# S5 woven with HGRN, retention last, and the output projection's rows parted to match

## The chip, the cores and the metric

The kernel runs on one core of one Trainium2 chip. The metric is device time in microseconds: three runs of the kernel before took 3756.23, 3757.74 and 3765.32 us, median 3757.74. One further execution was profiled; it took 3765.03 us.

## The reference

Two layers of a hybrid block over 256 context and 1024 latent tokens of width 1024, in float32. Each layer normalizes, projects once, runs four mixers in both directions on 256 channels each, projects their joined outputs back, and ends with an MLP:

```python
pc, pl = split_cols(hc @ w_in), split_cols(hl @ w_in)
a_c, a_l = hgrn2_mixer(pc[0], pl[0], lb, hg_norm_g)
r_c, r_l = retention_mixer(pc[1], pl[1], ret_log_gamma, pos_c, pos_l)
g_c, g_l = gdn_mixer(pc[2], pl[2], rows, conv_w, a_log, dt_bias, gdn_norm_g)
s_c, s_l = s5_mixer(pc[3], pl[3], lam_re, lam_im, log_dt, b_re, b_im, c_re, c_im, d_skip, glu_w, glu_b)
y_l = jnp.concatenate([a_l, r_l, g_l, s_l], axis=-1) @ w_out
y_c = jnp.concatenate([a_c, r_c, g_c, s_c], axis=-1) @ w_out if need_ctx else None
```

The second layer needs no context output (`need_ctx` is false there). HGRN is gated linear attention in chunks of 16 with a decay for each channel. Retention turns q and k by rope, attends within chunks of 64 (joined to 128 here) with a fixed decay and carries a state. S5 is a complex diagonal scan over 16 groups of 16 channels; its sum over both directions goes through GELU and a gated linear unit. Gated delta (gdn) is the fourth.

## The kernel before, in words

Everything is transposed: channels on the 128 partitions, tokens along the free axis. The joined mixer output `a` is 8 rows of 128 channels in HBM: rows 0 and 1 are HGRN's, 2 and 3 retention's, 4 and 5 gated delta's, 6 and 7 S5's. A float32 product is made of three passes over a high and a low half (hi x hi, lo x hi, hi x lo), so a product over n rows takes 3n matmuls.

A mixer is a Python generator that writes its instructions in pieces. `piped` runs the segments of one mixer one piece apart, and `weave(a, b, n, c, m)` writes a piece of a, then n of b, then m of c. Program order is only a wish: a scheduler with a model of the engines puts the instructions of each engine in their final order, by priority and by when it thinks the inputs are there. Each engine then runs its queue in that order, and so does SyncE (SP), which issues nearly all DMAs.

In each layer, when the projection is done, the order is: the end of gated delta (`gdn_out`) woven with HGRN, retention (`ret`) woven with HGRN, S5 alone (`s5`), and the rest of HGRN and of the modulation (lines 1963 to 1971). `gdn_out` and `ret` share one pool of tiles (`rtp`), HGRN has its own on the right side, and S5's pool lies in the outer region `sl`. The modulation products (`mod`, 256 KB weight loads each) are woven in between.

`ret` works on segments of 256 tokens, five of them. It first loads its tables (`rt_tb`, line 335). Stage 1 loads v, x, a copy of x with swapped halves in four DMAs (`rt_xs`, line 356), and rope tables; ropes k on VectorE and GpSimd (lines 358 to 360), stores it, transposes it (372), scales it (377), multiplies it with v (386) into the states `rt_S`, which `chain` then scans (401). When all of stage 1 is done, stage 2 ropes q, multiplies q and k (422), masks (424), and adds products with v and with the states (434, 437); `gnorm` normalizes, gates and stores the rows of `a` (lines 71 to 112).

`s5` works in four quarters. A quarter loads tables of 1.15 MB, multiplies the inputs by them (`s_px`, 1365), turns them (1371 to 1375), scans (1380), turns back (1384 to 1395), and multiplies again (`s_py`, 1403 and 1405). After every second quarter come transposes (1422, 1429) and GELU (1441 to 1445); at the end the gated unit (1454 to 1460) and the stores.

The output projection is in two parts. Part 1 (low priority, `hiprio` down) loads six rows of `a` (`load_a`, tile `at`, line 1756), splits them (1757, 1758), and runs 8 x 3 groups of 18 matmuls (layer 1: 8 x 2) into `wo_ps`; each group adds the residual (1781) and stores to `xs`. Part 2 (called "few") does the two rows that are left with 6 matmuls a group on top of `xs`, and leads on to the norm and the MLP. Two lists, `rowsA` and `rowsB`, give the order in which the input projection makes its 128-column blocks; 'r' and 's' stand for retention's v and S5's input.

Of the kernel before, what the change touches and what calls it, by code (L numbers as in the profile page):

```python
# [146 lines left out]
def hgrn(k, l, need_ctx):  # L147
# [27 lines left out]
    def stage1(sg):  # L175
# [15 lines left out]
        if full:  # L191
# [8 lines left out]
            AD = tp.tile([128, 8, 64], F32, name='hg_ad', tag='hg_ad', bufs=2)  # L200
            A = tp.tile([128, 8, 2, 64], F32, name='hg_A', tag='hg_A', bufs=1)
            yield
# [3 lines left out]
        for li, s in enumerate((1, 2, 4, 8, 16, 32, 64)):  # L206
            nb = 256 // s
            if full:
# [5 lines left out]
                else:  # L214
                    for x in range(2):
                        nc.scalar.activation(A[Y2[x], :, 1 - x], ps[Y2[x]], AF.Copy)
                        nc.vector.tensor_copy(A[Y2[x], :, x], AD[Y2[x]])
# [1499 lines left out]
def within(k, gen, tp, tag):  # L1717

    while True:
        k.tp, k.mxt = tp, (tag, k.nps[tag])  # L1720
        try:
            next(gen)
        except StopIteration:
            return
        yield


def weave(a, b, n, c=(), m=0):

    for _ in a:  # L1730
        for _ in range(n):
            next(b, None)
        for _ in range(m):
            next(c, None)


def run(gen):
    for _ in gen:
        pass
# [128 lines left out]
def program(k):  # L1868
    from contextlib import ExitStack
    nc, tc = k.nc, k.tc  # L1870
    with ExitStack() as es:
        pool = lambda st, name, **kw: st.enter_context(tc.tile_pool(name=name, bufs=1, **kw))
        near = lambda st, name, **kw: pool(st, name, reuse_waits='tile', **kw)
# [60 lines left out]
        for l in range(2):  # L1934
            need = l == 0
            blocks = ALL if need else LAT
            xsrc = k.I['xT'] if l == 0 else xs
            k.mml = ('mm', 'mm', 'mo')
            k.g = {}
            k.rows_done.clear()  # L1940
            k.wpool, k.ecm = k.balance[0]
            k.filler = proj_steps(k, l, H, k.rowsA, need)
            drain(k)
            k.filler = proj_steps(k, l, H, k.rowsB, need)
            with ExitStack() as st:
                gv, gc, su, tb = (near(st, f'{n}{l}') for n in ('gv', 'gc', 'su', 'tb'))
                with hi():
                    for i, _ in enumerate(within(k, gdn_conv(k, l, need, gc, gv), su, 'mx')):
                        if i == k.statat:
                            gdn_stats(k, l)  # L1950
                    if l == 0:
                        hg_params(k)
                    run(within(k, s5_tables(k, l), tb, 'mc'))
            with ExitStack() as st, hi():
                gs, fp = near(st, f'gs{l}'), near(st, f'gf{l}')
                run(within(k, gdn_main(k, l, need, fp), gs, 'mx'))
            drain(k)
            hs.close()
            hs = ExitStack()
            k.wpool, k.ecm = k.balance[1]  # L1960
            with ExitStack() as sl, ExitStack() as sr, hi():
                with ExitStack() as sh:
                    hg = within(k, hgrn(k, l, need), near(sh, f'hg{l}', side='right'), 'mx')
                    with ExitStack() as st:
                        rtp = near(st, f'rt{l}')
                        mod = (x for i, r in k.mods[l] for x in modulation(k, i, r, k.wp, (('w_hi', 'w_lo'), k.wb[1], 4)))
                        weave(within(k, gdn_out(k, l, need), rtp, 'mc'), hg, k.ratios[0], mod, k.mr[0])
                        weave(within(k, ret(k, l, need), rtp, 'mc'), hg, k.ratios[1], mod, k.mr[1])
                    weave(within(k, s5(k, l, need), near(sl, f's5{l}'), 'mc'), hg, k.ratios[2], mod, k.mr[2])
                    run(hg)  # L1970
                    run(mod)
                with ExitStack() as sa, tc.high_priority(offset=-k.hiprio):
                    wa = near(sa, 'wa', side='right')
                    k.mml = k.womm
                    pair = lambda: [wa.tile([128, T], F32R, name=n, tag='h', bufs=12) for n in ('ahi', 'alo')]
                    A = load_a(k, l, (4, 5, 2, 3, 0, 1), wa, k.nwa, blocks, pair)

                    def start(m, b0, bn):
                        x = wa.tile([128, 512], F32, name='xp', tag='t2', bufs=k.nwa)[:, :bn]
                        nc.sync.dma_start(x, xsrc[m, :, b0:b0 + bn])  # L1980
                        return x
                    run(w_out(k, l, A, blocks, start, lambda m, b0, bn, x: nc.sync.dma_start(xs[m, :, b0:b0 + bn], x)))
            k.hp = near(hs, f'hp{l}', side='right')
            k.mml = DENSE
            with ExitStack() as st:
                k.xp = k.np_ = near(st, f'ml{l}')
                t0 = blocks[0][0]
                Xt = [k.xp.tile([128, T], F32, name=f'x{i}') for i in range(8)]
                X = lambda kt: Xt[kt]
                part = lambda m, b0, bn: Xt[m][:, b0:b0 + bn]  # L1990
                pair = lambda: [k.xp.tile([128, T], F32R, name=n, tag='hid', bufs=k.nhid) for n in ('ahi', 'alo')]
                A = load_a(k, l, (6, 7), k.xp, k.nt2, blocks, pair)
                for b0, bn in blocks:
                    for kt in range(8):
                        nc.sync.dma_start(Xt[kt][:, b0:b0 + bn], xs[kt, :, b0:b0 + bn])
                new_acc = lambda: k.xp.tile([128, T], F32, name='nr_acc', tag='hid', bufs=k.nhid)
                acc = [new_acc()]
                H = [hpair(k) for _ in range(8)]

                def done(m, b0, bn, x):  # L2000
                    square(k, acc[0], x, m, b0, bn)
                    if m == 7:
                        norm_mod(k, X, acc[0], l, 3, b0, bn, H)
                run(w_out(k, l, A, blocks, part, done, True))
                if k.mods[2 + l]:
                    k.mml = DENSE2
                    k.filler = (x for i, r in k.mods[2 + l] for x in modulation(k, i, r, k.xp, ('w_mo', 2, 1)))
                H2 = [hpair(k) for _ in range(8)] if l == 0 else None

                def final(m, b0, bn):  # L2010
                    k.mml = DENSE
                    if (m, b0) == (0, t0):
                        acc[0] = new_acc()
                    sl = slice(b0, b0 + bn)
                    if m is not None:
                        square(k, acc[0], Xt[m][:, sl], m, b0, bn)
                        return
                    if l == 0:
                        norm_mod(k, X, acc[0], 1, 0, b0, bn, H2)
                        return  # L2020
                    rb = rnorm(k, acc[0], b0, bn)
                    for kt in range(8):
                        u = k.np_.tile([128, 512], F32, name='nm_u', tag='t2', bufs=k.nt2)[:, :bn]
                        nc.vector.scalar_tensor_tensor(u, Xt[kt][:, sl], k.vecs[:, 128 + kt:129 + kt], rb[:, :bn],  # L2024
                                                       op0=MULT, op1=MULT)
                        nc.sync.dma_start(k.O[kt, :, b0 - TC:b0 - TC + bn], u)
                mlp(k, l, H, X, blocks, final)
                if l == 0:
                    for kt in range(8):
                        nc.sync.dma_start(xs[kt], Xt[kt])  # L2030
                H = H2
# [7 lines left out]
def tune(k):  # L2039
    k.nps = dict(mm=2, mx=3, mc=2, mo=1)  # L2040
    k.nmc = 2
    k.mods = (((0, 1), (0, 2), (1, 0)), ((1, 1), (1, 2)), (), ())
    k.xat = 0
    k.bm = False
    k.gA, k.gM, k.gT, k.gQ = 3, 3, 2, 3
    k.nln, k.nvs = 3, 1
    k.hiprio = 6000
    k.convfirst = False
    k.cut = 8
    k.ratios = (1, 1, 1)  # L2050
    k.mr = (0, 1, 1)
    k.hlag = 9
    k.nw0 = 8
    k.parts = (1, 1)
    k.womm = ('mm', 'mx', 'mo')
    k.backat = 0
    k.rowsA = [16, 14, 17, 15, 'h', 18, 19]
    k.rowsB = ['r', 10, 11, 8, 9, 12, 13, 2, 3, 4, 5, 0, 1, 20, 21, 6, 7, 's']
    k.npace = {}
    k.lowprio = 8000  # L2060
    k.chainprio = 2000
    k.wb = (3, 4)
    k.nt2 = 5
    k.sqp, k.nva, k.nlp = (1, 4), (0, 2, 4, 6), (1, 3, 4, 5, 7)
    k.nz = 6
    k.nwa = 8
    k.balance = ((1, 4), (3, 4))
    k.nhid = 6
    k.ncv, k.ntk, k.statat = 4, 3, 3
    k.nv = (2, 2)  # L2070
    k.mods = (((0, 1), (0, 2), (1, 0)), ((1, 1), (1, 2)), (), ())
    k.hlag = 8
    k.nlp = (2, 4, 6)
# [29 lines left out]
```

## Time and profile before

| | us |
|---|---|
| median of three runs | 3757.74 (3756.23 to 3765.32) |
| profiled execution | 3765.03, its span 3763.2 |
| TensorE busy over the span | 3351.4 (89%) |
| VectorE, ScalarE, GpSimd | 2089.8, 1115.8, 1149.9 |
| HGRN woven with retention | 665 to 872 and 2591 to 2800 |
| S5, with part 1 of the output projection | 872 to 1059 and 2800 to 2978 |
| part 2, norm, first MLP matmuls | 1059 to 1131 and 2978 to 3034 |

In the rows below, a stretch lists for each engine its busy time and its instructions in brackets, in the order TensorE, its weight load, VectorE, ScalarE, GpSimd; then the mean granted TensorE clock (1 is 2.4 GHz), the busy share of the DMA engines and GB/s. A group of instructions gives line, engine, operation, output and input, shapes and count, then busy time and mean duration, and behind the second bar the engine's idle time ahead of it and what ended it. SPq is SyncE's queue.

### The profile page before, as it was taken

The numbers are of one execution on the slowest core, as the hardware profiler recorded it, in microseconds if no ns is written. First come the engines' busy times: TensorE is split into PE (matmuls) and PEld (weight loads), VectorE is DVE, ScalarE is ACT, GpSimd is POOL, SyncE is SP. The second block draws the span as 40 slices with busy tenths as digits, with TensorE's granted clock in tenths as the row PEclk, the third lists the DMA queues.
The fourth block names the chain that finished last, engine by engine and source line by source line (L and its number), as shares of the span: only waits on it lengthen the run. The fifth ranks groups of instructions, "written<-read, shape, count | busy, mean of one in ns | idle before, by whom it ended". The sixth has DMA issues, their size and how long they took to land. (4 is left out here: it accounts for less than half of the span.)

```text
span 3763.2 us, 59989 instructions
## 1 busy us (share of the span) xinstructions
PE 3351.4 (89%) x23367; PEld 2718.6 (72%) x23367; DVE 2089.8 (56%) x3927; ACT 1115.8 (30%) x1991; POOL 1149.9 (31%) x1198
## 2 busy tenths in 40 slices
PE   5888999787879999999998886997678599999997
PEld 3777788555758888888886775776457478888886
DVE  9978521885664433443447977413956654344445
ACT  5333221663143112112114342213542232222222
POOL 3753332562222111111114853323532131111111
PEclk8889999898989999999999998998889799999998
DMA  5666544966321111111113566436735211111111
GB/s 205 191 175 186 143 123 132 299 204 208 126 98 40 36 40 37 40 40 39 36 40 109 179 189 174 138 109 219 234 105 187 93 43 48 48 48 46 51 45 65
DMA packets 423948, 429.44 MB, mean 114 GB/s; under 512 B 185968, under 2 KB 299504, under 8 KB 422640
## 3 DMA queue, kind: packets, MB, share of 16 engines
q1 hardware_dynamic: 404224, 399.13, 34.5%
q10 hardware_dynamic: 19440, 26.48, 2.0%
q8 instruction: 184, 3.01, 0.3%
q14 instruction: 100, 0.82, 0.1%
HBM read 313.26 MB, written 112.22 MB: 113 GB/s over the span
## 5 line engine op out<-in xcount | busy, mean ns | idle before, releaser
L1521 PE MATMUL dn_ps<-hid,w_hi 128*128 128x512 f32 (+1 forms) x2560 | 729.0, 373 | 7.4 <-DVE x L1834 7.1
L1834 DVE SCALAR_TENSOR_TENSOR x<-dn_ps,mod,x 128x512 f32<-128x512 f32 (+1 forms) x640 | 433.1, 695 | 325.3 <-PE dn_ps L1521 324.8
L1506 POOL TENSOR_TENSOR w_lo<-w_st,w_hi 128x512 fp32r<-128x512 f32 (+1 forms) x212 | 291.5, 1378 | 1038.5 <-ACT w_hi L1503 987.3
L1521 PEld LDWEIGHTS dn_ps<-hid,w_hi 128*128 128x128 f32 x2560 | 463.8, 189 | 97.6 <-DVE x L1834 8.5
L1503 ACT ACTIVATE w_hi<-w_st 128x512 fp32r<-128x512 f32 (+1 forms) x408 | 249.2, 620 | 809.3 <-PE dn_ps L1521 276.2
L1521 PE MATMUL up_ps<-hlo,w_hi 128*128 128x512 f32 (+1 forms) x1280 | 476.1, 372 | 3.5 <-DVE hlo L1631 1.9
L1521 PE MATMUL up_ps<-hhi,w_hi 128*128 128x512 f32 (+1 forms) x1280 | 476.5, 373 | 2.0 <-ACT hhi L1630 2.0
L1521 PE MATMUL up_ps<-hhi,w_lo 128*128 128x512 f32 (+1 forms) x1280 | 476.1, 372 | 0.0
L1521 PE MATMUL dn_ps<-hid,w_lo 128*128 128x512 f32 (+1 forms) x1280 | 469.3, 373 | 0.0
L1663 PE MATMUL pj_ps<-hhi,w_hi 128*128 128x512 f32 (+1 forms) x960 | 360.7, 377 | 48.0 <-ACT w_hi L1503 34.7
L1663 PE MATMUL pj_ps<-hlo,w_hi 128*128 128x512 f32 (+1 forms) x960 | 363.8, 379 | 3.2 <-DVE hlo L1631 3.2
L1663 PE MATMUL pj_ps<-hhi,w_lo 128*128 128x512 f32 (+1 forms) x960 | 360.9, 378 | 2.5 <-POOL w_lo L1506 2.5
L1819 POOL TENSOR_TENSOR up_q<-up_r 128x256 f32<-128x256 f32 (+1 forms) x160 | 155.7, 973 | 567.5 <-ACT up_r L1818 477.5
L1506 DVE TENSOR_TENSOR w_lo<-w_st,w_hi 128x512 fp32r<-128x512 f32 (+1 forms) x196 | 147.3, 756 | 314.2 <-ACT w_hi L1503 303.6
L1521 PEld LDWEIGHTS up_ps<-hlo,w_hi 128*128 128x128 f32 x1280 | 242.4, 189 | 49.3 <-DVE hlo L1631 3.6
L1521 PEld LDWEIGHTS up_ps<-hhi,w_hi 128*128 128x128 f32 x1280 | 242.3, 189 | 46.5 <-ACT hhi L1630 2.9
L1521 PEld LDWEIGHTS dn_ps<-hid,w_lo 128*128 128x128 f32 x1280 | 241.0, 189 | 46.0
L1521 PEld LDWEIGHTS up_ps<-hhi,w_lo 128*128 128x128 f32 x1280 | 242.3, 189 | 44.1
L1821 DVE TENSOR_TENSOR hid<-up_q,hid 128x256 fp32r<-128x256 f32 (+1 forms) x160 | 113.5, 718 | 279.7 <-ACT hid L1820 277.5
L1663 PEld LDWEIGHTS pj_ps<-hhi,w_hi 128*128 128x128 f32 x960 | 188.1, 196 | 82.0 <-ACT w_hi L1503 36.3
L1820 ACT ACTIVATE hid<-up_q 128x256 fp32r<-128x256 f32 (+1 forms) x160 | 89.2, 584 | 421.6 <-PE dn_ps L1521 337.5
L1663 PEld LDWEIGHTS pj_ps<-hlo,w_hi 128*128 128x128 f32 x960 | 187.8, 196 | 36.0 <-DVE hlo L1631 4.5
(401 smaller groups left out, 5904.4 us busy)
## 6 DMA issues: line engine op xcount, KB each, us to landing
w_st<-in_w SPq DMA_DIRECT2D x256, 256.0 KB
w_mo<-in_mod_w SPq DMA_DIRECT2D x160, 256.0 KB
w_st<-in_w_ch SPq DMA_DIRECT2D x88, 256.0 KB
z<-pj_z ACTq DMA_DIRECT2D x66, 256.0 KB
gd_KV<-kv SPq DMA_DIRECT2D x80, 192.0 KB
s_ta<-s5t SPq DMA_DIRECT2D x8, 1152.0 KB
w_mo<-in_mod_w SPq DMA_DIRECT2D x16, 512.0 KB
at<-a SPq DMA_DIRECT2D x32, 256.0 KB
```

Of the source, the lines that this page charges most:

```text
L1503: nc.scalar.activation(fl(hi), fl(st), AF.Copy)
L1506: eng.tensor_tensor(fl(lo), fl(st), fl(hi).bitcast(F32), op=SUB)
L1521: k.nc.tensor.matmul(out, w, x, start=(i + j == 0), stop=(i == n - 1 and j == 2))
L1663: nc.tensor.matmul(ps[:, :n], x, y, start=(kt == 0 and i == 0), stop=(kt == 7 and i == 2))
L1819: nc.gpsimd.tensor_tensor(q[:, :bn], r[:, :bn], r[:, :bn], op=MULT)
L1820: nc.scalar.activation(hi[:, sl], q[:, :bn], AF.Copy)
L1821: nc.vector.tensor_tensor(lo[:, sl], q[:, :bn], hi[:, sl].bitcast(F32), op=SUB)
L1834: nc.vector.scalar_tensor_tensor(X(m)[:, sl], ps[:, :bn], g, X(m)[:, sl], op0=MULT, op1=ADD)
```

## The change

S5 gets a pool of its own that is closed before retention's is opened; it is woven with what is left of HGRN after `gdn_out`. Retention then runs by itself, with only modulation pieces beside it, from a pool in the region where S5's was. Part 1 of the output projection takes rows 4, 5, 0, 1, 6, 7 instead of 4, 5, 2, 3, 0, 1, and part 2 takes retention's rows 2, 3 instead of 6, 7. The projection makes S5's input first and retention's blocks last.

```diff
--- before.py
+++ after.py
@@ -1962,18 +1962,19 @@
                 with ExitStack() as sh:
                     hg = within(k, hgrn(k, l, need), near(sh, f'hg{l}', side='right'), 'mx')
                     with ExitStack() as st:
-                        rtp = near(st, f'rt{l}')
+                        rtp = near(st, f'go{l}')
                         mod = (x for i, r in k.mods[l] for x in modulation(k, i, r, k.wp, (('w_hi', 'w_lo'), k.wb[1], 4)))
                         weave(within(k, gdn_out(k, l, need), rtp, 'mc'), hg, k.ratios[0], mod, k.mr[0])
-                        weave(within(k, ret(k, l, need), rtp, 'mc'), hg, k.ratios[1], mod, k.mr[1])
-                    weave(within(k, s5(k, l, need), near(sl, f's5{l}'), 'mc'), hg, k.ratios[2], mod, k.mr[2])
+                    with ExitStack() as st:
+                        weave(within(k, s5(k, l, need), near(st, f's5{l}'), 'mc'), hg, k.ratios[1], mod, k.mr[1])
                     run(hg)
+                    weave(within(k, ret(k, l, need), near(sl, f'rt{l}'), 'mc'), hg, 0, mod, k.mr[2])
                     run(mod)
                 with ExitStack() as sa, tc.high_priority(offset=-k.hiprio):
                     wa = near(sa, 'wa', side='right')
                     k.mml = k.womm
                     pair = lambda: [wa.tile([128, T], F32R, name=n, tag='h', bufs=12) for n in ('ahi', 'alo')]
-                    A = load_a(k, l, (4, 5, 2, 3, 0, 1), wa, k.nwa, blocks, pair)
+                    A = load_a(k, l, (4, 5, 0, 1, 6, 7), wa, k.nwa, blocks, pair)
 
                     def start(m, b0, bn):
                         x = wa.tile([128, 512], F32, name='xp', tag='t2', bufs=k.nwa)[:, :bn]
@@ -1989,7 +1990,7 @@
                 X = lambda kt: Xt[kt]
                 part = lambda m, b0, bn: Xt[m][:, b0:b0 + bn]
                 pair = lambda: [k.xp.tile([128, T], F32R, name=n, tag='hid', bufs=k.nhid) for n in ('ahi', 'alo')]
-                A = load_a(k, l, (6, 7), k.xp, k.nt2, blocks, pair)
+                A = load_a(k, l, (2, 3), k.xp, k.nt2, blocks, pair)
                 for b0, bn in blocks:
                     for kt in range(8):
                         nc.sync.dma_start(Xt[kt][:, b0:b0 + bn], xs[kt, :, b0:b0 + bn])
@@ -2055,7 +2056,7 @@
     k.womm = ('mm', 'mx', 'mo')
     k.backat = 0
     k.rowsA = [16, 14, 17, 15, 'h', 18, 19]
-    k.rowsB = ['r', 10, 11, 8, 9, 12, 13, 2, 3, 4, 5, 0, 1, 20, 21, 6, 7, 's']
+    k.rowsB = ['s', 2, 3, 4, 5, 0, 1, 20, 21, 6, 7, 'r', 10, 11, 8, 9, 12, 13]
     k.npace = {}
     k.lowprio = 8000
     k.chainprio = 2000
```

SyncE's queue in layer 0 before, where HGRN ends (`hg_oq` are HGRN's rows, `at` the loads of part 1, `s_ta` a table of S5):

```order
L112 DMA a_75<-hg_oq 128x2x256
L81 DMA gn_gate<-z_69 128x2x256
L1330 DMA s_in<-zs_77 32x8x64
L1330 DMA s_in<-zs_77 128x8x64 x2
L112 DMA a_75<-hg_oq 128x2x256 x2
L1756 DMA at<-a_75 128x256
L1756 DMA at<-a_75 128x512 x2
...
L1347 DMA s_ta<-s5t_83 128x2304
L1980 DMA xp<-in_xT 128x256
```

And after, where S5 ends (`s_th` are S5's rows 6 and 7, `rt_` retention's tiles, `kr` its roped k in HBM):

```order
L1460 DMA a_75<-s_th 128x512 x2
L1756 DMA at<-a_75 128x512
L335 DMA rt_tb<-rtb_85 128x1032
L344 DMA rt_v<-zr_73 128x2x256
L352 DMA rt_x<-z_69 128x2x256
L356 DMA rt_xs<-z_69 32x2x256 x4
L357 DMA rt_tab<-in_rtab 128x2x256
...
L81 DMA gn_gate<-z_69 128x2x256
L352 DMA rt_x<-z_69 128x2x256
L1756 DMA at<-a_75 128x512
L357 DMA rt_tab<-in_rtab 128x2x256
```

Before, all loads of part 1 stand together behind HGRN's last store. Now those of rows 6 and 7 follow S5's stores, and the last of them stands behind 47 rows (73 DMAs) of retention; in layer 1 behind 44 rows (70 DMAs).

TensorE in layer 0 before, where part 1 begins, beside S5's first quarter:

```order
L1365 MATMUL s_px<-s_u,s_ta 64x128
L1403 MATMUL s_py<-s_u,s_tb 128x160
L1405 MATMUL s_py<-s_h,s_tb 128x160
L1403 MATMUL s_py<-s_u,s_tb 128x160
L1405 MATMUL s_py<-s_h,s_tb 128x160
L1521 MATMUL wo_ps<-ahi,w_hi 128x256 x2
L1521 MATMUL wo_ps<-ahi,w_hi 128x512 x3
L1521 MATMUL wo_ps<-alo,w_hi 128x256
```

And after, behind S5's gated unit, where five groups of part 1 are open:

```order
L1521 MATMUL wo_ps<-ahi,w_lo 128x512
L372 MATMUL rt_pt<-c_ident,rt_x 128x128 x8
L386 MATMUL rt_pk<-rt_v,rt_kt 64x64 x16
...
L372 MATMUL rt_pt<-c_ident,rt_x 128x128 x4
L386 MATMUL rt_pk<-rt_v,rt_kt 64x64 x32
L422 MATMUL rt_pa<-rt_qz,rt_kr 128x256 x8
L434 MATMUL rt_po<-rt_A,rt_v 64x128 x2
L437 MATMUL rt_po<-rt_qd,rt_S 64x128 x2
...
L1521 MATMUL wo_ps<-ahi,w_hi 128x512 x2
L1521 MATMUL wo_ps<-alo,w_hi 128x512
```

Part 1 lay beside S5's quarters before. Now 90 of its 432 matmuls (layer 1: 78 of 288) stand ahead of retention, then all five stage 1 blocks and the first segment of stage 2 without one between, and the others beside the rest of stage 2 and behind it.

On VectorE, S5 comes in at HGRN's 50th of 279 VectorE instructions in layer 0, and its last quarter runs on past HGRN's last norms. In layer 1 it comes in at the 108th of 251, with two of its quarters ahead of HGRN's end.

## Rows read from the trace of the kernel before

**Rows 1.** Stretches: from:to, length, busy us (and instructions) of each engine, TensorE clock, DMA.

```profile
665.00:872.00 207.00, 166.10 (x1990) 107.25 (x1990) 179.12 (x360) 128.15 (x212) 116.97 (x117) 0.91 0.73 238
872.00:1059.00 187.00, 147.47 (x882) 117.88 (x878) 110.95 (x215) 50.86 (x95) 39.57 (x43) 0.85 0.49 159
1014.00:1037.00 23.00, 9.78 (x70) 8.48 (x67) 16.57 (x36) 0.78 (x3) 5.43 (x7) 0.66 0.12 39
2591.00:2800.00 209.00, 150.92 (x1720) 99.70 (x1719) 157.97 (x326) 107.95 (x180) 112.97 (x113) 0.83 0.59 191
2800.00:2978.00 178.00, 120.85 (x672) 93.45 (x672) 102.00 (x191) 41.71 (x73) 35.26 (x42) 0.80 0.46 149
2938.00:2961.00 23.00, 9.77 (x75) 8.40 (x72) 15.81 (x34) 0.89 (x3) 5.42 (x6) 0.60 0.14 44
1059.00:1131.00 72.00, 54.64 (x260) 44.52 (x261) 50.90 (x85) 33.10 (x63) 20.11 (x17) 0.86 0.33 110
2978.00:3034.00 56.00, 43.36 (x171) 33.65 (x172) 37.97 (x55) 24.98 (x41) 14.65 (x11) 0.86 0.34 118
```

**Rows 2.** Groups on VectorE, 665 to 872 us: count, busy us, mean ns.

```profile
L401 DVE SCALAR_TENSOR_TENSOR rt_S<-rt_S,rcd 128x64 f32<-128x64 f32 x36 | 17.3, 519 | 0.0
L360 DVE TENSOR_TENSOR rt_x<-rt_x,rt_xs 128x512 f32<-128x512 f32 x10 | 8.2, 820 | 0.0
L358 DVE TENSOR_TENSOR rt_x<-rt_x,rt_tab 128x512 f32<-128x512 f32 x10 | 7.8, 775 | 0.0
L424 DVE TENSOR_TENSOR rt_A<-rt_pa,rt_tb 128x512 f32<-128x512 f32 x10 | 6.8, 678 | 0.0
L377 DVE TENSOR_TENSOR rt_kt<-rt_pt,rt_tb 128x512 f32<-128x512 f32 x10 | 6.4, 676 | 0.0
```

**Rows 3.** Line 356: duration in ns, least/median/most, first and last start.

```profile
L356 SPq DMA_DIRECT2D rt_xs<-z x76: 302/424/2280, 633.5 to 2728.5; - x76
```

**Rows 4.** Timeline 642 to 647 us: start, duration, instruction, idle before.

```profile
642.73 0.58 SPq L357 DMA_DIRECT2D rt_tab<-in_rtab  x1
646.48 1.27 POOL L359 TENSOR_TENSOR rt_xs<-rt_xs,rt_tab 128x512 f32<-128x512 f32 x1 [1.38 <-DMA rt_tab<-in_rtab]
```

**Rows 5.** Stretches as in rows 1, w_out's own instructions (tile wo_ps) alone.

```profile
897.00:1014.00 117.00, 91.60 (x432) 72.11 (x432) 15.32 (x24) 0.94 0.53 173
2825.00:2930.00 105.00, 73.56 (x288) 54.53 (x288) 11.91 (x16) 0.89 0.53 167
```

**Rows 6.** Groups on TensorE, 665 to 872 us.

```profile
L437 PE MATMUL rt_po<-rt_qd,rt_S 64*64 64x128 f32 x144 | 13.2, 300 | 0.0
L422 PE MATMUL rt_pa<-rt_qz,rt_kr 128*128 128x256 f32 x40 | 11.4, 425 | 0.7 <-ACT rt_qz L413 0.7
L434 PE MATMUL rt_po<-rt_A,rt_v 128*64 128x128 f32 x80 | 10.0, 327 | 4.0 <-DVE rt_A L424 4.0
L105 PE MATMUL gn_rb<-c_ident,gn_r 128*64 128x128 f32 x176 | 13.6, 303 | 1.9 <-POOL gn_r L97 1.9
```

**Rows 7.** Chain of waits, layer 1: start, us, what.

```profile
2960.19 0.67 PE s_pw L1422 x4
2969.41 7.13 PE s_pg L1454 x12
2977.28 0.70 DVE s_th L1459
2978.49 2.62 DMA at<-a
2981.82 18.02 PE wo_ps L1521 x66
```

**Rows 8.** Timeline of TensorE, layer 0, w_out's second part begins.

```profile
1062.39 2.07 PE L1521 MATMUL wo_ps<-ahi,w_hi 128*128 128x256 f32 x8 [6.04 <-ACT ahi L1757]
```

**Rows 9.** Groups on VectorE, 872 to 1059 us.

```profile
L1387 DVE TENSOR_TENSOR s_x<-s_x,s_ta 128x318 f32<-128x318 f32 x8 | 8.4, 1054 | 4.4 <-POOL s_t L1384 4.4
L1386 DVE TENSOR_TENSOR s_x<-s_x,s_ta 128x318 f32<-128x318 f32 x8 | 3.8, 475 | 0.0
```

## The prediction

> **What bounds the kernel now.** I read the table by stages first (busy time of each engine in stretches cut where one stage hands over to the next), then the groups of instructions on VectorE and TensorE inside those stretches, then single times from the timeline and the chain of waits. The projections and the MLP, where TensorE is close to full, are not touched. All that moves lies between the end of the projections and the first MLP matmul: 665 to 1131 us in layer 0 and 2591 to 3034 us in layer 1 [rows 1].
>
> That stretch has three parts. HGRN woven with retention takes 207 us; VectorE is busy for 179 of them (86%), TensorE for 166, GpSimd for 117: VectorE sets the pace in layer 0, and loosely in layer 1 (158 of 209). S5 comes next, alone among the mixers: 187 us, VectorE 111, TensorE 147, of which 91.6 are w_out's first part [rows 1, 5]. S5 is not limited by an engine here. The stretch cut to one S5 quarter without w_out beside it is 23 us long, VectorE busy for 16.6 and TensorE for 9.8 [rows 1], and the chain of waits goes matmul, multiply, scan, GpSimd, multiply, matmul through it and then through transposes, GELU and GLU to the last store [rows 7]. At the end w_out's second part needs S5's last rows: chain 2960.19 (last quarter over), 2977.28 (GLU's last product), 2978.49 (load of the stored rows), 2981.82 (first matmul) [rows 7]; 1062.39 in layer 0 [rows 8]. So before, w_out's first part costs nothing (it lies beside S5), and S5's latency is paid almost whole.
>
> The change puts S5 in the long weave and retention where S5 was. The time at which w_out's second part starts, "few" below, tells the result: 1062.4 and 2981.8 now.
>
> **HGRN's weave.** Retention's VectorE rows in layer 0 sum to 46.5 us (17.3 + 8.2 + 7.8 + 6.8 + 6.4) [rows 2]. S5 gives back 16.6 per quarter [rows 1]. By the order of layer 0, quarters 0 to 2 and half of the last lie before HGRN's last norms: 3 x 16.6 = 49.8, +3. I take 875 for the end instead of 872. In layer 1 S5 comes in only at HGRN's 108th of 251 VectorE instructions, and two quarters (2 x 15.8 = 31.6) get in for about 45 out; at 76% busy I give back 10 of the 13: 2790 instead of 2800. Bounds: 862 to 900, and 2782 to 2810.
>
> Here the place to look is the shared use of memory by VectorE and GpSimd. The row shows 1054 ns for S5's multiply that runs beside a GpSimd multiply and 475 ns for its twin right behind it [rows 9]. The Trainium skill ("SBUF — State Buffer", section "Who interferes with whom") says that a VectorE instruction with two SBUF inputs and a GpSimd instruction that reads SBUF contend, and that the second one fully blocks; the row agrees. That speaks against the change: by the rule S5 meets more of this where GpSimd is busy 117 of 207 us than where it was busy 40 of 187. But retention leaves 56 instructions of that kind (rt_S 36, the two rope lines 20) and three quarters bring some 54, so the sum above stays; the case where it does not is a rival below.
>
> **S5's end.** Layer 0: the rest of the last quarter, 23 alone [rows 1], up to 41 beside w_out's groups ((187 - 22)/4). Only some five groups of w_out are ready there, so I take 28, and the finish as before, 1037 to 1059 = 22: 925, instead of 1059. Layer 1: two quarters at 26 and the finish of 18 (2960.2 to 2978.5): 2790 + 70 = 2860, instead of 2978. Bounds 23 to 41 for each quarter. S5 is 134 and 118 us earlier; that is the gain to be spent.
>
> **What is late next: retention.** Its tables lie where S5's tiles were, so its first load stands behind S5's last store on SyncE; nothing of it is prefetched. Before w_out can go on, two things must pass. On SyncE the last `at` load of row 7 stands behind 73 (layer 1: 70) DMAs of retention: at 424 ns [rows 3] that is 31 and 30 us of bare issue. A load takes 3.2 us to land: issued until 643.31, the GpSimd multiply that waits for it starts at 646.48 [rows 4]. On TensorE all five stage 1 blocks and the first segment's products stand ahead of the next w_out matmul. Five ropes through two buffers (landing 3.2, GpSimd 1.28 [rows 4], two adds and multiplies of .8 [rows 2], 2.1 of four more issues) cost some 8 to 9 each if nothing overlaps: 43, and with the second landing and the scan over S at the end 60. Bounds 31 and 60; I take 45, in each layer, with TensorE all but idle.
>
> After that TensorE has w_out's rest and retention's stage 2 to do. Of w_out's 432 matmuls (144 narrow ones count half: 360 units, 91.6 us, so 0.254 each [rows 5]) 90 stand before retention (42 narrow, 48 wide: 69 units), 291 units are left: 74.0 us. Layer 1: 78 of 288 done, 210 x 0.255 (73.6/288) = 53.6. Retention's share: its products 11.4 + 13.2 + 10.0 = 34.6 over five segments, four of them here, 27.7, and its norm matmuls (40 of 176 gn_rb rows: 13.6 x .23 = 3.1, and some 2 in front): 33 [rows 6]; three of four segments and norms in layer 1: 25. Retention was hidden on TensorE before, now it is not, and S5's own matmuls no longer lie beside w_out.
>
> Layer 0: 925 + 45 + 74 + 33 = 1077, against 1062.4: +14.6. Layer 1: 2860 + 45 + 53.6 + 25 = 2983.6, plus 4 for the last norm, store and load, since the order leaves no w_out matmul of the first part behind retention's last products there: 2987.6 against 2981.8: +5.8.
>
> **The second part, and the rest.** Few came behind a stretch at clock .60 to .66 [rows 1] and took 18.02 us for its first 66 wide matmuls, .273 each [rows 7], 0.02 more than in part one. With TensorE busy right before it this comes back: 120 x .02 and 96 x .02, -2 each. Against it its residual loads queue behind retention's stores, +1 each. The other order of the projection's rows moves the same matmuls; I cost it at nothing, since TensorE is busy through it (bounds -5 to +5).
>
> Sum: 14.6 + 5.8 - 4 + 2 = +18 us. The profiled execution took 3765.0 (3763.2 of span and 1.8 around it), so its counterpart would be 3783; the median of the runs is 7.3 below the profiled one, and the prediction goes by it: 3757.7 + 18 = 3776.
>
> **Rivals.**
> A, forecast: the wait for retention's stage 1 eats S5's earlier end, 3776. Chance .44. For it: the two queue positions. Against it: +18 is the small difference of 250 us saved and 270 spent, each end of stage 1 alone moving it by 30.
> B, faster: stage 1 runs at SyncE's issue rate. 31 + 3 instead of 45 twice, -22, and retention's matmuls overlap with w_out's as they do with each other (40 rt_pa rows at 425 ns are 17 us, in 11.4 of busy time [rows 6]): a third of its 58 us hidden, -19: 3735. If the late load did not hold up w_out at all it would be 3757.7 + 18 - 90 = 3686, which the order speaks against. For it: retention alone finds GpSimd, ScalarE and DMA free (DMA share .14 in S5's end [rows 1]). Chance .28.
> C, slower: S5 in the weave stretches HGRN. Place: VectorE from 700 to 875 and 2690 to 2790. S5's instructions on two memory inputs take 8.4 us of a quarter's 16.6, and the pair of rows 9 shows 2.2 times the time when GpSimd reads beside them; if most do, 5 quarters x 8 us x .8 (VectorE's busy share) = +32: 3808. It decides once VectorE is over 95% busy there. Against it: retention's rows carry the same waits already (rt_S at 519 ns [rows 2]). Chance .14.
> D, nothing to measure: retention's tail is exactly as long as the S5 time that it replaces (133 us in layer 0, 120 in layer 1 instead of 152 and 128): 3758. Chance .14.
>
> A difference under 0.3% (11 us) can't be told from none here. Of A some .10 falls within it and .03 below it, of B .04, of D .09 within and .03 on the fast side. Faster: .24 + .03 + .03 + .01 = .31; same .10 + .04 + .09 = .23; slower the remaining .46. Single bounds summed as independent (15 twice for stage 1, 20 for the weave, 15 for the quarters, 12 for TensorE's rest) give some 35 either way around A; taken to B and past C's middle: 3715 to 3822. Around A alone 3750 to 3805.
>
> **What would show it.** S5's last store at 925 and 2860 (C: 20 and 12 later), retention's first load right behind it; on TensorE a hole of some 45 us with only retention's short blocks (B: under 35); its first w_out matmul after that waiting for row 7's load; few's first matmul at 1077 and 2988; VectorE at 86% in the weave, with rt_S gone and s_h in its place. I am wrong if the hole is small, or if few starts before 1062 and 2982 in spite of it.

## The result, and the profile after

The changed kernel took 3797.91 us (median of 4 runs, 3795.41 to 3801.47), the kernel before 3761.53 in the same comparison: ratio 1.0089, 95% interval 1.0077 to 1.0101, slower by 33 us by that ratio (36 between the medians). The prediction was 3776, +18. Direction and range held. The size did not, and the experiments show that it came out of two errors of opposite sign: the new order of the mixers costs three times what I computed (59 us), and the new order of the projection's blocks, which I had put at nothing, gives almost half of it back (25).

The stretches of the changed kernel, cut where its stages hand over (length, busy time of TensorE, its weight load, VectorE, ScalarE, GpSimd, then clock, DMA share, GB/s):

```profile
664.00:868.00 204.00, 151.47 (x1656) 100.68 (x1656) 172.07 (x369) 122.57 (x206) 100.18 (x116) 0.86 0.62 201
868.00:936.00 68.00, 46.57 (x262) 34.98 (x263) 39.59 (x80) 23.81 (x45) 14.44 (x16) 0.80 0.34 109
936.00:991.00 55.00, 28.20 (x235) 19.85 (x234) 37.46 (x73) 9.71 (x16) 19.79 (x13) 0.65 0.85 256
991.00:1092.00 101.00, 101.00 (x696) 78.75 (x695) 31.25 (x54) 21.95 (x41) 28.71 (x22) 0.97 0.55 174
2624.00:2801.00 177.00, 123.70 (x1350) 82.29 (x1350) 145.05 (x308) 100.76 (x169) 84.68 (x104) 0.84 0.57 188
2801.00:2882.00 81.00, 50.06 (x287) 35.97 (x288) 52.11 (x99) 22.06 (x37) 22.03 (x22) 0.79 0.23 74
2882.00:2939.00 57.00, 34.52 (x265) 24.36 (x264) 39.03 (x74) 9.81 (x16) 18.33 (x13) 0.61 0.83 262
2939.00:3016.00 77.00, 70.30 (x469) 52.95 (x467) 21.77 (x35) 16.88 (x31) 21.97 (x17) 0.99 0.50 163
```

Four stages a layer where there were two [rows 1]: HGRN with S5, S5's rest, a hole, and a full TensorE. HGRN's weave did not stretch: 204 us with VectorE busy for 172 (84%), 207 and 179 before. In the third stage TensorE works for 28 of 55 us, and all of it but 3.6 us is retention's own. In the fourth it is busy without a gap, in layer 1 up to the wait just ahead of part 2. Part 2 of the output projection starts at 1091.7, 29 us later than before (1062.4, [rows 8]). In layer 1 the same four stages take 392 us from the end of the projection (2624) to part 2 (3016); before it was 391 (2591 to 2982). So by the trace nearly the whole loss arises in layer 0: 29 of the 34 us between the two profiled spans.

The hand-overs are where the order had them. SyncE's queue in layer 0, with S5's last stores, retention's first load behind them, and the last load of row 7:

```profile
934.27 1.63 SPq L1460 DMA_DIRECT2D a<-s_th  x2
936.86 0.32 SPq L1756 DMA_DIRECT2D at<-a  x1
937.27 0.38 SPq L335 DMA_DIRECT2D rt_tb<-rtb  x1
...
983.26 0.34 SPq L1756 DMA_DIRECT2D at<-a  x1
```

And TensorE, which goes on with part 1 only behind retention's first segment:

```profile
991.64 0.69 PE L437 MATMUL rt_po<-rt_qd,rt_S 64*64 64x128 f32 x4
992.26 1.22 PE L1521 MATMUL wo_ps<-ahi,w_hi 128*128 128x512 f32 x2
```

The row 7 load was issued at 983, and the low half made from it was written by VectorE from 990.53 to 991.2; TensorE came to part 1 at 992.26. So the two gates that the prediction named opened within 1 us of each other, and the trace alone can't say which of them counts. In this hole (the stretch in which part 1's matmuls stand still) GpSimd waits for retention's loads between 936 and 991 (waiting line, releaser, us in total, times, longest; the longest began at 925, in S5's finish):

```profile
POOL rt_xs L359 <- DMA rt_tab<-in_rtab: 36.4, 7, 19.9
```

These waits alone do not set its length. In layer 1 the chain of waits that ended last goes through the hole. Of its 36 us from 2896.4 to 2932.4 three DMAs take 12.9, and the last of them has landed at 2915.5; from there on the chain stands on VectorE, and then on retention's first products:

```profile
2911.24 4.23 DMA rt_tab<-in_rtab
...
2915.50 0.70 DVE rt_x L358
...
2932.38 0.70 PE rt_po L434 x4
```

Later in layer 1 the same chain goes through retention's last norm into part 2, as [rows 7] went through S5's gated unit:

```profile
3003.96 3.43 PE wo_ps L1521 x16
3007.39 3.01 issue
3010.40 1.27 POOL rt_o L109
...
3012.47 2.88 DMA at<-a
...
3016.05 17.82 PE wo_ps L1521 x66
```

One thing was new. In layer 0 S5's finish (transposes, GELU, gated unit, stores), from its last `s_py` at 902.5 to the end of the last store's issue, took 33.5 us; it was 22 before. TensorE there:

```profile
905.69 1.03 PE L1422 MATMUL s_pw<-c_ident,s_yy 128*32 128x128 f32 x8
...
911.12 0.28 PE L1521 MATMUL wo_ps<-ahi,w_lo 128*128 128x256 f32 x1
911.33 0.68 PE L1429 MATMUL s_pu<-c_ident,s_w 32*128 32x32 f32 x8
...
915.42 1.04 PE L1422 MATMUL s_pw<-c_ident,s_yy 128*128 128x128 f32 x8
917.19 1.09 PE L1429 MATMUL s_pu<-c_ident,s_w 128*128 128x128 f32 x8 [0.74 <-ACT s_w L1424]
919.02 2.05 PE L1454 MATMUL s_pg<-s_xg,s_gw 128*128 128x256 f32 x6 [0.74 <-ACT s_xg L1433]
```

Between S5's transposes stand runs of part 1's matmuls, so its chain waits in TensorE's queue.

### The profile page after: what moved, and what is told of

Its sections match the earlier page's. It is cut to its first block, busy times and chain, and to the rows that moved or that the text cites. A ratio compares the mean times of both kernels' runs of the same rounds, so it can differ in the third digit from the quotient of the medians.

```text
span 3796.9 us, 60029 instructions
## 1 busy us (share of the span) xinstructions
PE 3375.5 (89%) x23367; PEld 2733.0 (72%) x23367; DVE 2081.7 (55%) x3927; ACT 1114.2 (29%) x1991; POOL 1145.1 (30%) x1198
## 5 line engine op out<-in xcount | busy, mean ns | idle before, releaser
L1506 POOL TENSOR_TENSOR w_lo<-w_st,w_hi 128x512 fp32r<-128x512 f32 (+2 forms) x212 | 287.5, 1359 | 1014.6 <-ACT w_hi L1503 985.7
L1663 PEld LDWEIGHTS pj_ps<-hhi,w_lo 128*128 128x128 f32 x960 | 188.3, 197 | 37.5 <-POOL w_lo L1506 5.8
```

Of the source, the lines that this page charges most:

```text
L1506: eng.tensor_tensor(fl(lo), fl(st), fl(hi).bitcast(F32), op=SUB)
L1663: nc.tensor.matmul(ps[:, :n], x, y, start=(kt == 0 and i == 0), stop=(kt == 7 and i == 2))
```

## The experiments

All ratios are against the kernel before, run beside each of them; the changed kernel stands at 1.0089. Left-out lines of the diffs are marked by dots.

**One layer changed at a time.** Which layer loses? Choosing by `need` (true in layer 0) between the two orders, the two row sets, and the two projection lists:

```diff
+ if need:      # layer 0 as changed
+     with ExitStack() as st:
+         weave(within(k, s5(...), near(st, f's5{l}'), 'mc'), hg, k.ratios[1], mod, k.mr[1])
+ else:         # layer 1 as before
+     weave(within(k, s5(...), near(sl, f's5{l}'), 'mc'), hg, k.ratios[2], mod, k.mr[2])
...
```

> Layer 0 as in the changed kernel (its projection order too), layer 1 as before. Theory, from the two traces: the loss arises in layer 0 alone (part 2 starts 32 us later there, 1094 instead of 1062), so about +32 us against before, 3793. Rival, the terms of the prediction (layer 0 +13, layer 1 +5): +13, 3775.

> Layer 1 as in the changed kernel, layer 0 as before. Theory: S5's earlier end and retention's tail cancel in layer 1, +1 us against before, within 5 us of 3761. Rival: half of the loss belongs to layer 1 (it only looks late in the trace because layer 0 delays it): +15 or more.

Measured: layer 0 alone 3799.2, ratio 1.0095 (1.0079 to 1.0112); layer 1 alone 3762.5, ratio 0.9998 (0.9988 to 1.0007). The trace was read rightly: layer 0 holds all of the loss, and in layer 1 the change as a whole costs nothing. That it is a sum of a loss and a gain there came out only later.

**Part 1's rows loaded ahead of retention.**

```diff
-                    weave(within(k, ret(k, l, need), near(sl, f'rt{l}'), 'mc'), hg, 0, mod, k.mr[2])
-                    run(mod)
-                with ExitStack() as sa, tc.high_priority(offset=-k.hiprio):
+                with ExitStack() as sa:
                     wa = near(sa, 'wa', side='right')
...
                     A = load_a(k, l, (4, 5, 0, 1, 6, 7), wa, k.nwa, blocks, pair)
+                    weave(within(k, ret(k, l, need), near(sl, f'rt{l}'), 'mc'), hg, 0, mod, k.mr[2])
+                    run(mod)
+                    sa.enter_context(tc.high_priority(offset=-k.hiprio))
```

> The changed kernel with the loads of part 1's rows (tile at) written ahead of retention at its priority, so that the last load of row 7 follows S5's last store on SyncE; the rest of part 1 stays at low priority. Theory A: the late row 7 load holds part 1 up, and with it early the hole of 55 us is filled: 30 us gained in each layer, 3738. Theory B: behind it stand the residual loads (xp) and weights of part 1 on SyncE and the order on TensorE; only the three groups go ahead that stand ahead of stage 1 in the new order, 5 to 10 us in each layer, 3783.

Measured: 3808.1, ratio 1.0116 (1.0101 to 1.0131), no gain at all, but a loss of some 10 us. Theory A fell: with the row 7 load in front, three more groups ran ahead (the gap between part 1's matmuls begins at 951 instead of 941), and it is still 50 us long. Theory B's gain did not come either: part 2 starts at 1095. The late row 7 load alone is not what holds part 1 up; its residual loads still stand behind retention on SyncE (the first is issued at 995.6) and its matmuls behind stage 1 on TensorE. A run with the residual loads early as well, and retention's tiles left in their place, was not made.

**S5's rows first in part 1's sums**, so that no matmul of part 1 can stand inside S5's finish.

```diff
+    order = kts if few else sorted(kts, key=lambda i: (i < 6, i))
...
-        yield from mm3(..., [W[m, kt] + (A[kt][0][:, sl], A[kt][1][:, sl]) for kt in kts])
+        yield from mm3(..., [W[m, kt] + (A[kt][0][:, sl], A[kt][1][:, sl]) for kt in order])
```

> The changed kernel with part 1 of the output projection summing over S5's rows 6 and 7 first, so that none of its matmuls can stand between those of S5's finish. Theory: in layer 0 S5's finish took 34.5 us instead of 22 because 63 matmuls of part 1 stand between its transposes on TensorE; S5's last store comes 10 us earlier, at about 926, and the moved matmuls (63, in layer 1 60) cost their 14 us later: about +4 in layer 0 and +14 in layer 1 against the changed kernel, 3815. Rival: the finish is slow for another reason (ScalarE, the clock), S5's end stays at 936: +14 in both, 3825.

Measured: 3805.2, ratio 1.0103 (1.0086 to 1.0120). The finish is short again; TensorE in layer 0, from the last quarter's end at 905 on:

```profile
904.79 0.91 PE L1422 MATMUL s_pw<-c_ident,s_yy 128*32 128x128 f32 x6
906.38 0.68 PE L1429 MATMUL s_pu<-c_ident,s_w 32*128 32x32 f32 x8 [0.68 <-ACT s_w L1424]
907.30 1.09 PE L1422 MATMUL s_pw<-c_ident,s_yy 128*128 128x128 f32 x8 [0.24 <-ACT s_xg L1433]
909.13 1.09 PE L1429 MATMUL s_pu<-c_ident,s_w 128*128 128x128 f32 x8 [0.74 <-ACT s_w L1424]
910.96 2.05 PE L1454 MATMUL s_pg<-s_xg,s_gw 128*128 128x256 f32 x6 [0.74 <-ACT s_xg L1433]
```

From the first transposes to the gated unit 6 us, 13 in the changed kernel; S5's last store at 928 instead of 936 although its last quarter ended 2 us later. So the runs of part 1 cost S5's end 10 us, as the theory has it. Little of it arrives: part 2 of layer 0 starts at 1089, 2 us earlier than in the changed kernel, and the kernel as a whole is no faster.

**Retention without its loads of swapped halves.**

```diff
-        for y in range(2):
-            for hf in range(2):
...
-                nc.sync.dma_start(xs[a:a + 32], src[:, b:b + 32, :]...)
...
-        nc.gpsimd.tensor_tensor(xs, xs, bc(tab[:, 1:2], [128, 2, 256]), op=MULT)
+        nc.gpsimd.tensor_tensor(xs, x, bc(tab[:, 1:2], [128, 2, 256]), op=MULT)
```

> The changed kernel without retention's 76 loads of swapped halves (rt_xs, 4 of 7 DMAs of a rope): the rope multiplies x itself by the second table, so rope's swap is left out of the computation. Theory: the hole on TensorE between S5's end and part 1's rest (55 us in each layer) is set by retention's transfers and their issue (DMA share .85 there), so it shrinks to some 42 and the kernel gains 20 to 26 us against the changed one, 3773. Rival: the hole is a chain over VectorE, TensorE and GpSimd from segment to segment, and it gains less than 8 us.

Measured: 3780.9, ratio 1.0043 (1.0028 to 1.0058), 17 us better than the changed kernel; a little less than expected, and not by the way that was expected. Layer 0 from 936 to 1079:

```profile
936.00:980.00 44.00, 35.23 (x298) 27.93 (x297) 30.62 (x58) 9.82 (x18) 13.77 (x11) 0.88 1.02 357
980.00:1051.00 71.00, 70.62 (x466) 55.60 (x464) 30.78 (x59) 15.86 (x29) 24.70 (x19) 1.00 0.50 158
1051.00:1079.00 28.00, 15.95 (x169) 10.45 (x167) 4.76 (x9) 4.55 (x10) 7.17 (x6) 0.78 0.24 76
```

The scheduler now put part 1's groups between stage 1's blocks, and with them row 7's load at 943 (983 in the changed kernel) and the residual loads behind it, so the hole is filled (TensorE busy for 35 of 44 us). The run thus changed the order as well as the transfers. But stage 1 did not get shorter (its last states at 980, 974 in the changed kernel), retention's last product comes at 1065 in both, and part 2 now waits for retention: 28 us in which part 1 is through. So the run does not settle whether stage 1 is bound by its transfers; in layer 1 of the changed kernel the chain shown above has none in the hole's second half. It shows that behind the hole there is a second limit, close to it.

**One pass of three in part 1**, to see that limit.

```diff
+    if one:
+        for i, (wh, wl, xh, xl) in enumerate(terms):
+            k.nc.tensor.matmul(out, wh, xh, start=(i == 0), stop=(i == n - 1))
...
```

> The changed kernel with one pass (hi x hi) of three in part 1 of the output projection; the two passes with a low half are left out of the computation there. Theory: behind the hole TensorE's sum of part 1's rest and retention's stage 2 sets the start of part 2 (103 of 103 us busy in layer 0), so two thirds of part 1's rest, 49 us in layer 0 and 36 in layer 1, go: 3713. Rival: retention's own chain, 129 us from S5's last store to its last product in the changed kernel and in the one without the swapped loads, is the floor behind it: part 2 cannot start before some 14 us after that, and the two layers gain 10 to 15 each, 3772.

Measured: 3737.8, ratio 0.9927 (0.9912 to 0.9942), between the two. Layer 0:

```profile
928.00:980.00 52.00, 23.48 (x211) 17.85 (x213) 34.90 (x64) 7.91 (x13) 18.31 (x13) 0.57 0.84 255
980.00:1041.00 61.00, 55.95 (x434) 39.84 (x434) 31.78 (x57) 19.55 (x37) 25.89 (x19) 0.92 0.85 283
```

Part 1 is done at 1024, and part 2 starts at 1054.8, 127 us behind S5's last store (928), where 156 were needed with all passes. These 127 us are retention's own time with a third of part 1 beside it, so an upper bound for retention alone. S5's store was 123 us earlier in the changed kernel than before. So in layer 0 retention takes about what S5's earlier end saves, and 29 us of part 1's work come on top.

**Retention's tiles where HGRN's were**, so that its loads and stage 1 need not wait for S5's end; then the same with part 1's rows loaded early.

```diff
-                    weave(within(k, ret(k, l, need), near(sl, f'rt{l}'), 'mc'), hg, 0, mod, k.mr[2])
-                    run(mod)
+                weave(within(k, ret(k, l, need), near(sr, f'rt{l}', side='right'), 'mc'), hg, 0, mod, k.mr[2])
+                run(mod)
```

> The changed kernel with retention's tiles where HGRN's were instead of where S5's were, so that its loads and stage 1 can start at HGRN's end and run beside S5's last quarter and finish. Theory: retention's stage 1 being behind S5's last store is the loss; stage 1 then ends about where S5 does (940 in layer 0, 2890 in layer 1), and part 1 (92 and 74 us, none of it done before) and retention's stage 2 (33 and 25) follow: part 2 starts at 1070 and 2965 (layer 0's gain taken off 2990), 25 us gained in each layer, 3748. Rival: the two mixers share SyncE, VectorE and TensorE so that S5's end moves back by as much as stage 1 moves ahead: no gain, 3797.

> Both: retention's tiles where HGRN's were, and part 1's rows loaded ahead of retention. Theory: part 1's groups stand between stage 1's blocks in the order, so that the two gains add up partly: 3735 to 3748, below the kernel before (3761). Rival: part 1's tiles now lie where S5's and HGRN's last were, so its first load waits for S5's end as well, and it is no better than the one without the early loads.

Measured: 3790.6, ratio 1.0068 (1.0053 to 1.0083), and 3767.2, ratio 1.0009 (0.9998 to 1.0020). Layer 0 of the second, from HGRN's end to part 2 (1073.6):

```profile
867.00:924.00 57.00, 35.02 (x226) 24.84 (x226) 40.09 (x72) 16.75 (x31) 21.41 (x21) 0.76 0.59 181
924.00:953.00 29.00, 20.52 (x199) 16.66 (x196) 23.43 (x50) 13.62 (x26) 2.98 (x2) 0.82 0.87 283
953.00:1073.00 120.00, 112.20 (x767) 87.28 (x766) 46.17 (x81) 22.82 (x42) 37.71 (x29) 0.99 0.52 167
```

The gap of 50 us between part 1's matmuls is gone in both kernels (9 us at most is left). The first gained less than expected, since part 1 now starts only at 960 in layer 0 and its 90 early matmuls are no longer ahead. The second takes back 31 us, nearly all of what the change cost, and did not get below the kernel before.

**The projection's order taken back, and alone.**

```diff
-    k.rowsB = ['s', 2, 3, 4, 5, 0, 1, 20, 21, 6, 7, 'r', 10, 11, 8, 9, 12, 13]
+    k.rowsB = ['r', 10, 11, 8, 9, 12, 13, 2, 3, 4, 5, 0, 1, 20, 21, 6, 7, 's']
```

> The changed kernel with the order of the input projection's blocks as before (retention's first, S5's last). Theory: that order costs nothing either way, since TensorE is busy through the projection: within 5 us of the changed kernel. Rival: it delays the gated delta mixer or HGRN's start, and taking it back gives or costs 8 us or more.

Measured: 3823.2, ratio 1.0157 (1.0140 to 1.0174). The rival was right: the old list costs the changed kernel 25 us. Of these, 6 lie ahead of part 2 in layer 0 (1098.1), 6 in layer 1, and 11 in layer 0's second part, where one residual load came late and TensorE stood still for 7 us (VectorE, with its idle time and what ended it):

```profile
1115.76 0.48 DVE L1781 SCALAR_TENSOR_TENSOR x<-wo_ps,mod,x 128x256 f32<-128x256 f32 x1 [3.97 <-DMA x<-xs]
```

The kernel before with the new list, the edit the other way round:

> The kernel before with the changed order of the input projection's blocks alone (S5's first, retention's last). Taking that order back cost the changed kernel 25 us. Theory: the order in which the mixers' inputs come must fit the order of the mixers, so here it costs about as much, +15 to +25, 3785. Rival: gated delta ends 20 us earlier by it whatever follows, and it gains: -5 to -15, 3752.

Measured: 3716.3, ratio 0.9868 (0.9854 to 0.9881), 50 us faster than before: both theories fell by their size, the first by its sign too. This is the fastest kernel of the study, from one line of the change. In layer 1, from the projection's end to part 2, 352 us instead of 391. SyncE's queue there, before and then with the new list, around S5's first load:

```profile
2799.98 0.36 SPq L112 DMA_DIRECT2D a<-rt_o  x1
2801.49 0.36 SPq L112 DMA_DIRECT2D a<-hg_oq  x1
2801.94 1.93 SPq L1330 DMA_DIRECT2D s_in<-zs  x3
```

```profile
2757.18 6.57 SPq L112 DMA_DIRECT2D a<-rt_o  x2
2764.17 1.91 SPq L1330 DMA_DIRECT2D s_in<-zs  x3
```

S5 stands behind retention's last store on SyncE (by the program its tiles come free only with retention's as well; the run does not part the two). With the new list its first load went 38 us earlier (gated delta ended 24 us earlier, at 2554), and its end followed, 2932 instead of 2978. In layer 0 S5's last quarter ended 19 us earlier (1017 instead of 1037), but only 9 us are left of it at part 2: its finish took 33 us instead of 22, with part 1's matmuls between its transposes again, as in the changed kernel:

```profile
1026.34 0.68 PE L1429 MATMUL s_pu<-c_ident,s_w 32*128 32x32 f32 x8
...
1030.95 0.39 PE L1521 MATMUL wo_ps<-ahi,w_lo 128*128 128x512 f32 x1
1031.18 1.04 PE L1422 MATMUL s_pw<-c_ident,s_yy 128*128 128x128 f32 x8
```

**S5's block alone moved to the front.**

```diff
-    k.rowsB = ['r', 10, 11, 8, 9, 12, 13, 2, 3, 4, 5, 0, 1, 20, 21, 6, 7, 's']
+    k.rowsB = ['s', 'r', 10, 11, 8, 9, 12, 13, 2, 3, 4, 5, 0, 1, 20, 21, 6, 7]
```

> The kernel before with S5's block alone moved to the front of the projection's second list; retention's blocks come next as before and HGRN's last. With the whole new list gated delta ended 15 and 24 us earlier, retention and with it S5 followed, and 50 us were gained. Theory: S5's block at the front is what lets gated delta end earlier; here too it ends near 612 and 2554, and the kernel takes 3716 to 3728. Rival: it is retention's blocks at the end; here gated delta ends at 627 and 2578, and the kernel stays within 6 us of 3765.

Measured: 3725.5, ratio 0.9892 (0.9875 to 0.9908): this one move has four fifths of the gain. The time is the theory's, its reason is not. Gated delta ended at 625 and 2569, hardly earlier in layer 0; in layer 1 the last of the projection's blocks, HGRN's here, were done later (2615 instead of 2591), and retention again had its last product 34 us earlier, perhaps because it had less of HGRN beside it. What the two lists have in common is retention's end in layer 1 (2750 and 2753 against 2787), reached by different ways. Which link of the order sets it was not isolated.

**The two better layers together.** Layer 0 as before, layer 1 with retention in HGRN's place and early loads (the two diffs above, chosen by `need`).

> Layer 0 as before; layer 1 as in the kernel with retention where HGRN's tiles were and part 1's rows loaded early, which took 372 us from the end of its projection to part 2, against 391 before and 392 changed. Theory: the layers add up, 19 us less than before, 3745. Rival: layer 1's gain hung on layer 0's new placement as well, within 6 us of before.

Measured: 3747.0, ratio 0.9952 (0.9940 to 0.9965). The layers add up; it beats both kernels, but not the kernel before with the new list.

## Why the prediction was right, and what was wrong in it

**The number.** +18 was computed for the new order of the mixers alone, with the projection's list at nothing. Measured: this order costs 59 us with the old list (3823.2 against 3764.2) and about 82 with the new one (3797.9 against 3716.3, not run beside each other); the new list gives 25 in the changed kernel and 50 in the kernel before. The case that was forecast came, a wait for retention that eats S5's earlier end. That the sign and the range held as well is luck, since two errors cancel: with the list alone put right, at -25, the same sum would have come to -7, a faster kernel.

**The step that failed outright**: "I cost it at nothing, since TensorE is busy through it (bounds -5 to +5)". TensorE is indeed full there either way (ahead of HGRN in layer 0 busy for 104.8 of 105 us before and 103.6 of 104 after). What the order of the blocks changes is not TensorE's sum but when each mixer can begin and end. In the kernel before S5 is queued behind retention, so that retention's end is passed on: 37 us in layer 1 became 38 at S5's first load and 46 at its last store. The wait to look at stood in the trace: S5's first load behind retention's last store.

**HGRN's weave**, 875 and 199 us into layer 1: measured 868 and 177. Rival C did not come: VectorE was busy for 84% in layer 0 (86 before) and 82% in layer 1 (76 before), and S5's multiply that took 1054 ns in [rows 9] took less in the weave:

```profile
L1387 DVE TENSOR_TENSOR s_x<-s_x,s_ta 128x318 f32<-128x318 f32 x6 | 4.1, 678 | 0.2 <-POOL s_t L1384 0.2
```

The prediction's count of 54 S5 instructions with two memory inputs leaves out S5's scans (8 a quarter, `s_x` from `s5r` and `s_x`, line 1380); the stage did not stretch in spite of them.

**S5's end**, 925: measured 936. The end of the last quarter was right (902.5, forecast 903), but by luck: the weave ended 7 us sooner and the quarter took 34 us behind it instead of 28. The step "the finish as before, 22" was off by 11; part 1's own matmuls in TensorE's queue lengthened it, and with them out of the way it was 23 again. In layer 1 the forecast was 269 us behind the projection's end (2860), and measured were 258 (2882), with the finish of 18 as forecast.

**The hole**, 45: measured 55 and 57. The place and the cause were right: retention begins behind S5's last store, and part 1 all but stands still. TensorE does not: retention's own matmuls keep it busy for about half of the hole. The size was 10 short in each layer, near the upper bound of 60, which counted the scan over the states; the chain shown above has VectorE, scan included, in the hole's second half. Of the two gates, the row 7 load turned out not to be the one that counts: with it early the gap was as long. Rival B, a short hole and retention's matmuls beside part 1's, had 41 us for both layers. The runs that come nearest to it got part of that: the hole filled gave 17 us, moved 7, moved with part 1's rows early 31; by the one-pass run retention's own 127 us stand behind it.

**TensorE's rest**, 107 and 79 + 4: measured 101 and 77. Right.

**The second part**, 2 us faster in each layer: this did not come. In layer 0 its first 11 us had a clock of 1.00 instead of .86, but from its first to its last matmul it took 47 us, 46 before. In layer 1 TensorE again stood still ahead of it, for 6.8 us; the clock of its first 18 us was .86, .85 before, and the first 66 matmuls took 17.8 us instead of 18.0.

**The layers.** Forecast +14.6 and +5.8; measured at the start of part 2 +29 and +1. The order of the mixers alone, read off the two pairs with the same list, costs 36 us in layer 0 and 7 in layer 1 with the old list, and 38 and 40 with the new one; with the old list another 11 lie in layer 0's second part. So the two edits do not simply add up. The list gains 39 us in layer 1 where S5 is queued behind retention, and 6 where it is not, and layer 1's +1 hides a loss and a gain of 7 or of 40 us each, by which edit is counted first.

## What to carry to other kernels

When a change has several edits, give each one a run of its own, the ones that look free first: here the edit that was costed at zero was the only one that gained, and the best kernel keeps only that one. Before a stage that leaves latency uncovered is swapped for another, compare what the two cost when they stand alone, with all their loads: retention took 127 us behind S5's end even with two thirds of part 1's matmuls out of its way, and S5's end had come 123 us earlier for it. And a new order in which inputs are produced is not free merely because the producing engine is full; follow each block to the first instruction that waits for it, and to the stage queued behind that.

## What the runs showed of the hardware

In the hole 14 MB moved at 256 GB/s with the DMA engines at a share of .85. Without the loads of 32 rows of swapped halves, and with part 1 running beside it, the same stage moved 357 GB/s at a share of 1.02. How much of that is the smaller loads' was not measured apart. The granted TensorE clock was .65 and .61 in the two holes and .57 in that of the one-pass kernel (1 is 2.4 GHz, .5 is 1.2), and .97 and .99 in the full stretches right behind the first two: part 1's rest paid almost nothing for the idle time ahead of it.
